# Layer norm with GELU: loads and stores on one DMA queue instead of two

## The chip, the cores and the metric

One NeuronCore of a Trainium2 chip; the other cores run nothing of this program. The metric is the device time in microseconds (us) of one execution. A kernel's time is the median over its timed runs. All runs compared here were in the fast state, at a granted clock of 1.0. Each of the last two experiments also had one run in the slow state, which is named there and left out. A *ring* is below what one queue has lined up on one of the 16 DMA engines; DMA engines are *in step* when they land a transfer at about the same time.

## The reference, cut to what matters

```python
# x: (8, 1024, 2048) float32; gamma, beta: (2048,)
mean = np.mean(x, axis=-1, keepdims=True)
var = np.var(x, axis=-1, keepdims=True)
out = gamma * (x - mean) / np.sqrt(var + eps) + beta
return 0.5 * out * (1 + np.tanh(np.sqrt(2 / np.pi) * (out + 0.044715 * out ** 3)))
```

67.1 MB are read and 67.1 MB are written.

## The kernel before

The 8192 rows are cut into 16 blocks of 4 MB (128 partitions, 4 rows of 2048 each). Five SBUF buffers hold blocks; a block is loaded, worked on in place and stored from the same buffer. SyncE issues the loads on its hardware DMA queue, ScalarE issues the stores on its own:

```python
def slot(b): return (b + SLOTS - 1) % SLOTS          # SLOTS = 5

# SyncE
for b in range(B):                                    # B = 16
    if stored(b):
        sy.wait_ge(s_store[s], stored(b))             # the buffer's last store has landed
    # b == 0 and b == SPLIT (3): four DMAs of one row per partition, else one of 4 MB
    sy.dma_start(out=xts[s], in_=xg[b]).then_inc(s_load[s], 16 * R)
...
# ScalarE, after the last GELU of block b
ins.then_inc(s_r, 1)
ac.dma_start(out=og[b], in_=xt)._wait_ge(s_r, b + 1).then_inc(s_store[slot(b)], 16)
ac.sem_inc(s_g, 1)
```

VectorE takes the statistics, GpSimd the reciprocal root, ScalarE normalises, VectorE multiplies by gamma, TensorE adds beta into PSUM, ScalarE applies GELU. The four rows of the last block are stored one by one.

## Time and profile before

| | before |
|---|---|
| median of 4 runs | 320.19 us (320.01 to 320.34) |
| span of the profiled run | 318.5 us |
| DMA queues, share of 16 engines | q1 (loads) 49.4%, q10 (stores) 49.0% |
| busiest compute engine | ScalarE 79% |

The prediction below quotes the page and the stretches. This is the DMA view of the kernel before from 304 us to the end of the span, in 40 slices of 0.36 us; the figures are GB/s.

```profile
GB/s 181 317 316 362 542 452 429 362 362 362 520 475 429 384 362 384 520 407 452 407 362 407 452 429 475 407 362 407 362 45 23 23 45 23 0 0 0 0 0 0
```

All 16 DMA engines work until about 314.5 us (29 slices). Then the rate is 23 to 45 GB/s. One engine alone moves an 8 KB packet in about 309 ns, 26.5 GB/s: what is left is one engine that is late. Its last packet ends at 316.57 us.

### The profile page before, as it was taken

To read this page: it belongs to the slowest core of one execution; us is meant where nothing else is said; L and a number is where in the kernel's file an instruction comes from. 1 tells how busy PE (TensorE), PEld (TensorE's weight loads), DVE (VectorE), ACT (ScalarE), POOL (GpSimd) and SP (SyncE) were. 2 spreads that over 40 slices of the span, in tenths; PEclk is the share of its full clock that TensorE was granted. 3 is DMA by queue.
4 is the path that set the end of the run, shared out by engine and by line. 5 is a ranking of instruction groups with operands and counts; after the bars stand their busy time and mean duration, and the time that the engine had idled before them with its cause. 6 is when DMAs were issued, how large, how long until landed. Compare 5 with 4: busy or idle time off the path is not lost.

```text
span 318.5 us, 2090 instructions
## 1 busy us (share of the span) xinstructions
PE 244.3 (77%) x520; PEld 57.2 (18%) x520; DVE 247.5 (78%) x386; ACT 251.7 (79%) x132; POOL 110.6 (35%) x201
## 2 busy tenths in 40 slices
PE   2769999999999989687795868958589595886860
PEld 1212222222212112111121112212112121111110
DVE  3499999999999897786968968599686986869810
ACT  2769999999999989698696967969589695995970
POOL 1144444444444444232443333333332433324300
DMA  7999999999999999999999999999999999999995
GB/s 289 438 457 401 394 434 430 444 424 436 432 424 444 417 453 416 440 440 416 457 403 457 420 436 444 411 461 403 453 432 424 449 407 457 424 432 403 453 396 209
DMA packets 6002, 134.26 MB, mean 421 GB/s; under 512 B 704, under 2 KB 752, under 8 KB 752
## 3 DMA queue, kind: packets, MB, share of 16 engines
q1 hardware_dynamic: 3168, 67.11, 49.4%
q10 hardware_dynamic: 2832, 67.13, 49.0%
q14 instruction: 2, 0.02, 0.0%
HBM read 67.13 MB, written 67.11 MB: 421 GB/s over the span
## 4 chain that ended last, share of the span: by engine, by line
DMA 64%; ACT 14%; DVE 10%; POOL 5%; PE 3%; issue 1%; ACTq 0%; DVEq 0%; POOLq 0%; SPq 0%
DMA xt<-in_x_dram 32%; DMA out_dram<-xt 30%; ACT yk L195 9%; DVE sts L149 7%; ACT xt L202 4%; POOL ves L135 3%; DVE zg L158 2%; PE ps L220 2%; DMA rows<-in_gamma_dram 2%; POOL rss L137 2%; POOL nms L139 1%; DVE mvs L155 1%; PE ps L237 1%; ACT g_t L191 1%; ACTq L205 0%
## 5 line engine op out<-in xcount | busy, mean ns | idle before, releaser
L149 DVE BATCH_NORM_STATS2 sts<-xt 128x6 f32<-128x512 f32 x256 | 157.7, 679 | 33.5 <-DMA xt<-in_x_dram 31.9
L195 ACT ACTIVATE yk<-xt,nms,rss 128x2048 bf16<-128x2048 f32 x64 | 133.7, 2090 | 48.9 <-POOL nms L139 42.9
L237 PE MATMUL ps<-zg,ident 128*128 128x512 bf16 x256 | 120.8, 627 | 55.8 <-DVE zg L158 54.7
L233 PE MATMUL ps<-b_hl,ones_b 33*128 33x512 bf16 x256 | 120.6, 624 | 2.2 <-PEq L228 2.2
L202 ACT ACTIVATE xt<-ps 128x2048 f32<-128x2048 f32 x64 | 118.9, 1858 | 1.5 <-PE ps L237 1.5
L135 POOL TENSOR_SCALAR ves<-mvs 128x1 f32<-128x1 f32 x64 | 38.5, 602 | 179.2 <-DVE mvs L155 179.2
L158 DVE TENSOR_TENSOR zg<-yk,g_t 128x2048 bf16<-128x2048 bf16 x64 | 76.5, 1195 | 19.2 <-ACT yk L195 19.2
L237 PEld LDWEIGHTS ps<-zg,ident 128*128 128x128 bf16 x256 | 27.6, 130 | 149.0 <-DVE zg L158 113.7
L233 PEld LDWEIGHTS ps<-b_hl,ones_b 33*128 33x128 bf16 x256 | 27.0, 127 | 92.1 <-issue 88.4
L139 POOL TENSOR_SCALAR nms<-mvs,rss 128x1 f32<-128x1 f32 x64 | 35.7, 558 | 6.3
L137 POOL TENSOR_TENSOR rss<-ves,mhalf 128x1 f32<-128x1 f32 x64 | 35.3, 552 | 5.3
L155 DVE BATCH_NORM_AGGREGATE mvs<-sts 128x2 f32<-128x24 f32 x64 | 16.9, 264 | 2.2
L220 PE MATMUL ps<-rows,ones 1*128 1x512 f32 x8 | 7.2, 1076 | 6.1 <-DMA rows<-in_gamma_dram 6.1
L188 ACT ACTIVATE b_hl<-rows 1x2048 bf16<-1x2048 f32 x1 | 1.9, 1909 | 5.3 <-DMA rows<-in_beta_dram 5.3
L166 DVE TENSOR_TENSOR b_hl<-rows,b_hl 1x2048 bf16<-1x2048 f32 x1 | 2.3, 2280 | 2.8 <-ACT b_hl L189 2.8
L220 PEld LDWEIGHTS ps<-rows,ones 1*128 1x128 f32 x8 | 2.5, 327 | 9.2 <-DMA rows<-in_gamma_dram 6.1
L191 ACT ACTIVATE g_t<-ps 128x2048 bf16<-128x2048 f32 x1 | 1.9, 1877 | 1.9 <-PE ps L220 1.9
L184 ACT ACT_TABLE_LOAD x1 | 1.3, 1283 | 0.9 <-SPq L107 0.9
L189 ACT ACTIVATE b_hl<-rows 1x2048 bf16<-1x2048 f32 x1 | 1.9, 1908 | 0.0
L161 DVE MEMSET b_hl<- 33x1024 uint32 x1 | 0.9, 912 | 1.2 <-SPq L107 1.2
L126 POOL MEMSET ones<- 65x128 f32 x1 | 0.2, 202 | 0.5 <-SPq L107 0.5
L130 POOL TENSOR_SCALAR_AFFINE_SELECT ident<-ident 128x128 bf16<-128x128 bf16 x1 | 0.3, 295 | 0.1
(7 smaller groups left out, 0.9 us busy)
## 6 DMA issues: line engine op xcount, KB each, us to landing
out_dram<-xt ACTq DMA_DIRECT2D x15, 4096.0 KB, 32.6
xt<-in_x_dram SPq DMA_DIRECT2D x14, 4096.0 KB
xt<-in_x_dram SPq DMA_DIRECT2D x8, 1024.0 KB, 8.4
out_dram<-xt ACTq DMA_DIRECT2D x4, 1024.0 KB, 8.6
rows<-in_beta_dram ACTq DMA_DIRECT2D x2, 8.0 KB, 5.9
rows<-in_gamma_dram ACTq DMA_DIRECT2D x1, 8.0 KB, 5.1
```

Of the source, the lines that this page charges most:

```text
L135: po.tensor_scalar(out=ves[:, c], in0=mvs[:, k, 1:2], scalar1=float(eps), scalar2=1.0, op0=ALU.add, op1=ALU.mult)._wait_ge(s_a, k + 1).the ...
L137: po.tensor_tensor(out=rss[:, c], in0=ves[:, c], in1=mhalf, op=ALU.pow)._wait_ge(s_q, 2 * k + 1).then_inc(s_q, 1)
L139: po.tensor_scalar(out=nms[:, c], in0=mvs[:, k, 0:1], scalar1=rss[:, c], scalar2=-1.0, op0=ALU.mult, op1=ALU.mult)._wait_ge(s_q, 2 * k + 2 ...
L149: ins = ve.bn_stats(out=sts[:, q, j, :], in_=xr[:, j, :])
L155: ve.bn_aggr(out=mvs[:, q], in_=sts[:, q])._wait_ge(s_o, count).then_inc(s_a, 1)
L158: ve.tensor_tensor(out=zgs[q % 2], in0=yks[q % 2], in1=g_t, op=ALU.mult)._wait_ge(s_n, count).then_inc(s_z, 1)
L191: ac.activation(out=g_t, in_=pss[0], func=ACT.Identity)._wait_ge(s_tg, 1).then_inc(s_c, 1)
L195: ac.activation(out=yks[t % 2], in_=xts[slot(b)][:, q], func=ACT.Identity, scale=rss[:, q:q + 1], bias=nms[:, q:q + 1])._wait_ge(s_p, t + ...
L202: ins = ac.activation(out=xt[:, q], in_=pss[i % 2], func=ACT.Gelu_apprx_tanh)._wait_ge(s_t, i + 1)
L220: ins = pe.matmul(pss[0][:, cols(j)], lhsT=ones[64:65], rhs=rows[64:65, j * K // nsub:(j + 1) * K // nsub, :d // K], start=True, stop=True)
L233: ins = pe.matmul(ps[:, cols(j)], lhsT=ones_b, rhs=b_hl[:, cols(j)], start=True, stop=False)
L237: ins = pe.matmul(ps[:, cols(j)], lhsT=ident, rhs=zgs[k % 2][:, cols(j)], start=False, stop=True)
```

## The change

All loads and all stores go to SyncE's queue, load b+4 behind store b; ScalarE issues no stores. Block 3's load becomes one DMA of 4 MB. The hardware loops of the other engines stay.

```diff
@@ SyncE
-                for b in range(B):
+                def load(b):
                     s = slot(b)
                     if stored(b):
                         sy.wait_ge(s_store[s], stored(b))
...
+                        sy.dma_start(out=xts[s], in_=xg[b]).then_inc(s_load[s], 16)
+                for b in range(SLOTS):
+                    load(b)
+                for b in range(B):
+                    s = slot(b)
+                    for q in range(R) if by_row(b) else (slice(None),):
+                        stores += 1
+                        c = slice(q, q + 1) if by_row(b) else q
+                        sy.dma_start(out=og[b, :, c], in_=xts[s][:, c])._wait_ge(s_r, stores).then_inc(s_store[s], 16)
+                    if SLOTS <= b + AHEAD < B:        # AHEAD = 4
+                        load(b + AHEAD)
@@ ScalarE
-                        ac.dma_start(out=og[b], in_=xt)._wait_ge(s_r, b + 1).then_inc(s_store[slot(b)], 16)
-                        ac.sem_inc(s_g, 1)
+                        ac.sem_inc(s_g, 1)._wait_ge(s_r, stores)
```

The intent: whole transfers in a row instead of loads and stores mixed by packets, and a ScalarE free of DMA issues.

More of the change, by code (lines that the diff above doesn't have):

```diff
@@ L12 @@
 SLOTS = 5
-SPLIT = 3
+AHEAD = 4
 K = 16
@@ L111, in _ @@
             def _(sy):
-                for b in range(B):
+                stores = 0
+                def load(b):
                     s = slot(b)
@@ L115, in _ @@
                         sy.wait_ge(s_store[s], stored(b))
-                    for q in range(R):
-                        if b == 0:
+                    if b == 0:
+                        for q in range(R):
                             sy.dma_start(out=xts[s][:, q:q + 1], in_=xg[0, :, q:q + 1]).then_inc(s_first[q], 16)
-                        elif b == SPLIT:
-                            sy.dma_start(out=xts[s][:, q:q + 1], in_=xg[b, :, q:q + 1]).then_inc(s_load[s], 16)
-                    if b not in (0, SPLIT):
-                        sy.dma_start(out=xts[s], in_=xg[b]).then_inc(s_load[s], 16 * R)
+                    else:
+                        sy.dma_start(out=xts[s], in_=xg[b]).then_inc(s_load[s], 16)
[9 more added lines that the diff above has]
+                        load(b + AHEAD)
             @block.gpsimd
@@ L152, in stats @@
                             if wait[0] is s_load[s]:
-                                ins.then_inc(s_load[s], -16 * R)
+                                ins.then_inc(s_load[s], -16)
                     ins.then_inc(s_o, 1)
@@ L175, in _ @@
                         s, q = divmod(k, R)
-                        stats(s, q, (s_load[s], 16 * R) if q == 0 else None, k + 1)
+                        stats(s, q, (s_load[s], 16) if q == 0 else None, k + 1)
                         scale((q - 1) % R, k + 1)
@@ L191, in _ @@
                 ac.activation(out=g_t, in_=pss[0], func=ACT.Identity)._wait_ge(s_tg, 1).then_inc(s_c, 1)
+                stores = 0
                 for t in range(T + 1):
@@ L202, in _ @@
                     ins = ac.activation(out=xt[:, q], in_=pss[i % 2], func=ACT.Gelu_apprx_tanh)._wait_ge(s_t, i + 1)
-                    if by_row(b):
+                    if by_row(b) or q == R - 1:
+                        stores += 1
                         ins.then_inc(s_r, 1)
-                        ac.dma_start(out=og[b, :, q:q + 1], in_=xt[:, q:q + 1])._wait_ge(
-                            s_r, b + q + 1).then_inc(s_store[slot(b)], 16)
-                        ac.sem_inc(s_g, 1)
-                    elif q == R - 1:
-                        ins.then_inc(s_r, 1)
-                        ac.dma_start(out=og[b], in_=xt)._wait_ge(s_r, b + 1).then_inc(s_store[slot(b)], 16)
-                        ac.sem_inc(s_g, 1)
+                        ac.sem_inc(s_g, 1)._wait_ge(s_r, stores)
                     else:
```

## The prediction

> **What bounds the kernel now.** I read the page first, busy shares, then the DMA queues, and after that the DMA traffic by stretch, the waits and the chain. No engine is the bound: the busiest three stand at 77 to 79%.
>
> ```profile
> PE 244.3 (77%) x520; PEld 57.2 (18%) x520; DVE 247.5 (78%) x386; ACT 251.7 (79%) x132; POOL 110.6 (35%) x201
> ...
> q1 hardware_dynamic: 3168, 67.11, 49.4%
> q10 hardware_dynamic: 2832, 67.13, 49.0%
> ...
> DMA 64%; ACT 14%; DVE 10%; POOL 5%; PE 3%; issue 1%; ACTq 0%; DVEq 0%; POOLq 0%; SPq 0%
> ```
>
> The two hardware queues (q1 holds SyncE's loads, q10 ScalarE's stores) together fill the 16 DMA engines for 98.4% of the span, half each, and the chain that ended last is 64% DMA. The question is thus only how fast the 16 engines drain 134 MB, and whether they are ever without work. The windows view, by stretch, tells both; its last two columns are the DMA share (over 1.00 by rounding of packets into stretches) and GB/s.
>
> ```profile
> 10.00:32.00 22.00, 16.43 (x33) 3.78 (x32) 17.81 (x26) 16.54 (x9) 6.95 (x12) 1.00 1.01 432
> 32.00:52.00 20.00, 18.38 (x41) 4.20 (x40) 18.76 (x31) 18.83 (x11) 7.98 (x13) 1.00 1.02 416
> 56.00:280.00 224.00, 179.55 (x388) 41.43 (x388) 185.28 (x293) 185.59 (x98) 83.22 (x145) 1.00 1.00 433
> 284.00:304.00 20.00, 14.69 (x33) 3.34 (x32) 15.43 (x24) 15.37 (x9) 6.54 (x12) 1.00 0.98 419
> 304.00:314.00 10.00, 3.73 (x9) 0.81 (x8) 1.22 (x1) 4.81 (x3) 0.00 (x0) 1.00 0.98 407
> 314.00:318.50 4.50, 0.00 (x0) 0.00 (x0) 0.00 (x0) 0.00 (x0) 0.00 (x0) 1.00 0.12 49
> ```
>
> From 10 to 32 us there are loads alone, on one queue: 432 GB/s. From 56 to 280 loads and stores alternate from two queues: 433 GB/s. So **one queue already runs as fast as two**. The slower stretches have causes of their own, treated below. The waits say how the queues are fed:
>
> ```profile
> SPq L122 <- DMA out_dram<-xt: 240.3, 11, 47.2
> ...
> DVE sts L149 <- DMA xt<-in_x_dram: 31.9, 11, 3.7
> ```
>
> SyncE spends 240 us waiting for a buffer's store to land before it reloads the buffer (11 times, blocks 5 to 15), and VectorE waits for 11 loads, 31.9 us in all. These waits look like an expensive loop: in the chain a store of 35 us, a load of 34 us, and 8.9 us of compute make 78 us for four blocks, 19.5 us a block. But the 35 and 34 us are queueing: about 3.5 transfers of 4 MB share engines that are busy all the time. The waits are the bound's shadow, not the bound.
>
> **The service time of one block.** The trace's packets of 32 KB take 1213 ns in mean as loads and 1215 ns as stores. A 4 MB transfer is 128 such packets, 8 on each DMA engine, so 8 x 1.213 = 9.70 us; block 1's load landed at 22.6 us on most engines and block 2's at 32.4, which agrees. A block in and out is 19.4 us; the landings into one buffer, five blocks apart, are 96.8 to 97.0 us apart, 19.4 per block. Compute needs less: ScalarE issued its first three stores at 36.02, 52.40 and 68.79 us, 16.4 us a block, while nothing held it up.
>
> **What the Trainium skill says.** "DMA: Bandwidth & Descriptors", section "Issuing engines are not separate DMA queues", says that DMAs of all issuing engines run on the same 16 DMA engines and interleave, and that several issuers save only sequencer time. The 432 against 433 GB/s agree. The same page, section "Queues, rings and completion order", says that each DMA engine alternates between the queues that have work by packets, and consumes one queue's descriptors in ring order. Both agree: a lone load takes 9.7 us here, and one among stores 30 us and more. That section also says that a completion's semaphore write lands only after that engine's earlier writes; the trace shows no stop for it between two loads (9.7 us apart) or between the stores of blocks 12 and 13 (285.1 to 294.8, 9.7 us). The page's table "Specifications" gives 435 GB/s as the fabric's ceiling: the trace's 432 to 433 is nearly that, so I leave no room for a faster transfer.
>
> **The change, part by part.**
> (1) *Stores move to SyncE's queue.* The same 19 store issues leave ScalarE, 339 ns each by the tile view, 6.4 us in all. ScalarE isn't the bound and waits for GpSimd 42.9 us in the kernel before; worth 0 on the path. SyncE has the time.
> (2) *Order.* Transfers are now strictly in a row: store b, load b+4, store b+1, load b+5. Bytes are the same, and so is packet time. Worth 0 if the queue never runs dry.
> (3) *Does it run dry?* I lay out the queue with 9.70 us per transfer. Loads 1 to 4 end at 22.7, 32.4, 42.1, 51.8; store 0 is issued at 36 and runs 51.8 to 61.5; store 1, issued at 52.4, runs to 71.2. Load 5 needs store 0 landed, with about 1 us for the slowest engine (the late landings of the trace): issued near 62.5, it has 8.7 us to spare, where an issue needs about 1 us to its first packet (first issue 0.93 us, first packet 1.92). Store 2 is computed at 68.8, needed at 80.9; store 3 at 85.2, needed at 100.3. Later a load is issued when the store of the block before lands, always with a load and a store (19.4 us) still ahead of it. A block's last row passes VectorE only after the next block's load has landed: store b can be issued 8.9 us after load b+1 (128.89 to 137.79 in the chain). In the new order four transfers, 38.8 us, lie between load b+1's end and store b's start. So the smallest slack is 8.7 us and the queue doesn't run dry.
> (4) *Block 3's load as one DMA in place of four.* Its 8 KB packets, 512 of them, took 10.76 us of each engine (mean 336 ns, beside the first store); as 32 KB packets it takes 9.70. This is the 416 GB/s of the stretch 32 to 52. Gain 1.06 us, on the bound.
> (5) *The tail.* Block 14's store was issued at 293.91, when block 13's was about to land (294.8 on most engines), and landed at 304.9: 10.1 us in place of 9.7, the DMA share of 0.98 in that stretch. In the new order load 15 ends at 275, so store 14 can be issued near 284 and is needed at 294: gain 0.4 us. The last block's rows are ready by 300 and needed from 304; four rows of 8 x 312 ns each are 10.0 us as before.
> (6) *The end.* One DMA engine is late: fifteen end by 314.7, the last at 316.57, and the span closes at 318.5. The same engine serves the same share: unchanged, 0.
>
> Sum: 320.14 - 1.06 - 0.4 = **318.7 us**.
>
> **The rivals.**
> *A. A bubble at every change of direction.* The kernel before has no ring on which a load follows a store: only load after load, store after store, or the two from different rings, where one ring's latency can hide behind the other's packet. With 13 or so loads among stores there are about 24 such changes. If each cost 0.3 us, it would be +7.2 us: 326 us, just slower than 2%; at 0.05 us, 1.2 us, 320. Against it: same-direction neighbours show no bubble though they too carry a semaphore write, and the alternating stretch runs full while changing direction at each packet. The trace can't exclude it, so it gets the tail of the range.
> *B. Head-of-line blocking.* SyncE stands at a store's wait while a load behind it could go. In the layout of (3) the slack is 8.7 us at the worst place. If compute were slower by more than that, the DMA would idle. Compute keeps 16.4 us against 19.4, so the lead grows until loads hold it. It would give 0 to +2 us if the start were tighter than laid out.
> *C. The stores and loads no longer fight, so the chain's 35 us becomes 10 and the kernel gets 20 us faster.* Transfers will land faster one by one, and waits on them will shrink, but the 98% share says that the engines have nothing to give. 134.2 MB at 433 GB/s are 310 us, plus 1.9 before the first packet, 1.9 for the late engine and 2.0 to the end: about 316, which is the floor of this program. A gain of 2% (313.7 us) is below it.
>
> **Range and chances.** The gains (4) and (5) sum to 1.5 us with little doubt about their size; the late engine may move by a microsecond either way; A at a few hundredths to 0.1 us adds up to 2.4. I put 8 times in 10 between 317.5 and 321.0. Faster by 2% would need what C lacks: 0.01. Slower by 2% (over 326.5) needs A at 0.3 us or more each, or B in every block: 0.04. Within 2%: 0.95.
>
> **What would show each step right or wrong.** In the DMA queues of the changed kernel one hardware queue should hold all 134 MB at 98 to 99%, and the other only gamma and beta. Issue to landing of a store should fall from a median of 32.6 us to 10 to 20. The stretch 32 to 52 should show about 432 GB/s, and 56 to 280 again 430 or more: a lower figure there is rival A if spread evenly over all blocks, rival B if idle stretches stand before late store issues on SyncE. VectorE's wait for loads should nearly vanish in the middle or just shift; it doesn't matter for the time. The prediction is wrong if a pair of store and load takes other than 19.4 us in the middle.

## The result, and the profile after

The changed kernel takes **322.01 us** (median of 4 runs, 321.26 to 322.72) against 320.19. The ratio is 1.0057, with a 95% interval of 1.0037 to 1.0077. Ratios here are the mean time of one kernel's fast runs over that of the other's of the same rounds, so not quite the ratio of the quoted medians. It is "the same" at the 2% level, but clearly slower, and outside the predicted range of 317.5 to 321.0.

The page of the changed kernel, for the lines that the prediction showed of the kernel before:

```profile
PE 244.3 (76%) x520; PEld 57.2 (18%) x520; DVE 248.2 (77%) x386; ACT 251.5 (78%) x132; POOL 113.4 (35%) x201
...
q1 hardware_dynamic: 5472, 134.22, 97.8%
q10 hardware_dynamic: 96, 0.02, 0.0%
...
DMA 47%; DVE 19%; ACT 15%; POOL 9%; PE 3%; issue 2%; SPq 0%; POOLq 0%; ACTq 0%; DVEq 0%
```

One queue carries everything and keeps the engines at 97.8%. The windows view, same stretches and columns as in the prediction (DMA share and GB/s last):

```profile
10.00:32.00 22.00, 16.42 (x33) 3.77 (x32) 17.86 (x26) 16.22 (x9) 6.95 (x12) 1.00 1.02 438
32.00:52.00 20.00, 18.38 (x41) 4.26 (x40) 18.76 (x31) 18.82 (x11) 8.03 (x14) 1.00 1.01 415
56.00:280.00 224.00, 184.01 (x398) 42.62 (x399) 187.85 (x295) 189.92 (x101) 87.19 (x148) 1.00 1.00 432
```

The middle runs at 432 GB/s, against 433. The stretch 32 to 52 is at 415 against 416: the slow spot that the prediction put down to the split load is still there **without the split load**. The waits of SyncE and VectorE:

```profile
SPq L122 <- DMA out_dram<-xt: 162.8, 11, 19.0
SPq L131 <- ACT xt L214: 126.0, 13, 30.8
...
DVE sts L160 <- DMA xt<-in_x_dram: 25.2, 9, 3.6
```

SyncE's waits for stores fell from 240 to 163 us, and its new waits for results are 126 us. Neither matters, since the queue had work all that time. The loss is at the end. The DMA view of the changed kernel from 304 us to the end, slices of 0.415 us:

```profile
GB/s 434 336 493 454 355 454 494 336 434 454 395 415 415 415 454 395 415 454 415 395 494 434 296 198 79 59 99 79 79 79 79 99 39 39 59 0 0 0 0 0
```

The common rate ends at about 313.7 us, *earlier* than before. But then some 79 GB/s go on for 3 us, and some 40 after that: 79 is three engines at 26.5 GB/s. Their last packets end at 317.37, 318.50 and 318.78 us. So the common end moved from about 314.6 to 313.7 us (-0.9), the distance from there to the last engine from 1.9 to 5.1 us (+3.2), and the span by +2.1 (318.5 to 320.6).

**When the lateness arises** can be read from the trace's landing records. Each large DMA here has 16 landing records, one per DMA engine; they don't say which engine. I call the last of the 16 minus their median the *lateness* of that DMA (L is a load, S a store, the number is the block), in us:

| | L2 | L4 | L8 | L12 | L15 | S14 |
|---|---|---|---|---|---|---|
| before | 0.63 | 1.03 | 1.03 | 1.71 | 2.24 | 2.22 |
| after | 0.83 | 2.05 | 3.03 | 4.11 | 4.90 | 4.95 |

In the changed kernel it grows throughout, and by steps. After 60 us, 44 of its packets took over 1253 ns (the usual 1213 and 40 more), 9.05 us too long in sum, which is about the drift of three engines. Of the 44, 24 end within 0.45 us before a load's landing: they are an engine's *last* packet of a load that stands before a store. Most of the others are one or two packets before that. Laid end to end, the packets form 16 chains, one per engine: some 35 of the 44, 7.0 us, lie on three of them. In the kernel before there are 17 such packets, 1.6 us in sum, and 1 of them ends a load.

The kernel before has another way to a late engine. Between 140 and 290 us it has no packet over 1253 ns, yet its lateness grows from 1.03 us at L8 to 2.24 at L15. The packets of 1216 to 1253 ns in that time make up for it: 106 packets, 62 of them of stores, 1.3 us too long in sum, most of them on one engine. What makes that engine a little slow is not known.

### The profile page after: what moved, and what is told of

It is laid out like the page before. It is cut to its first block, busy times and chain, and to the rows that moved or that the text cites. A ratio compares the mean times of both kernels' runs of the same rounds, so it can differ in the third digit from the quotient of the medians.

```text
span 320.6 us, 2087 instructions
## 1 busy us (share of the span) xinstructions
PE 244.3 (76%) x520; PEld 57.2 (18%) x520; DVE 248.2 (77%) x386; ACT 251.5 (78%) x132; POOL 113.4 (35%) x201
## 3 DMA queue, kind: packets, MB, share of 16 engines
q1 hardware_dynamic: 5472, 134.22, 97.8%
## 4 chain that ended last, share of the span: by engine, by line
DMA 47%; DVE 19%; ACT 15%; POOL 9%; PE 3%; issue 2%; SPq 0%; POOLq 0%; ACTq 0%; DVEq 0%
DMA out_dram<-xt 36%; DVE sts L160 12%; ACT yk L207 12%; DMA xt<-in_x_dram 9%; DVE zg L169 6%; POOL ves L146 5%; POOL rss L148 3%; PE ps L227 2%; ACT xt L214 2%; DMA rows<-in_gamma_dram 2%; POOL nms L150 1%; DVE mvs L166 1%; PE ps L244 1%; ACT g_t L202 1%; SPq L122 0%
## 5 line engine op out<-in xcount | busy, mean ns | idle before, releaser
L146 POOL TENSOR_SCALAR ves<-mvs 128x1 f32<-128x1 f32 x64 | 41.0, 641 | 171.4 <-DVE mvs L166 171.4
## 6 DMA issues: line engine op xcount, KB each, us to landing
out_dram<-xt SPq DMA_DIRECT2D x15, 4096.0 KB, 34.6
```

What stands on the lines that cost most here:

```text
L146: po.tensor_scalar(out=ves[:, c], in0=mvs[:, k, 1:2], scalar1=float(eps), scalar2=1.0, op0=ALU.add, op1=ALU.mult)._wait_ge(s_a, k + 1).the ...
```

## The experiments

The theories. **D**: on one ring, DMA engines that are a little behind the others lose time when they pass from a load to a store, so their lateness grows, and the last of them sets the end. **Step 4 of the prediction**: the split of block 3's load costs 1 us. **F**: one queue makes some engines late whatever the order. **I**: the lateness comes from loads issued on the landing of the slowest engine, with stores waiting behind them on SyncE. More came up on the way. Twelve kernels ran, all with correct results.

### Two queues, without the split

```diff
-                        elif b == SPLIT:
-                            sy.dma_start(out=xts[s][:, q:q + 1], in_=xg[b, :, q:q + 1]).then_inc(s_load[s], 16)
-                    if b not in (0, SPLIT):
+                    if b != 0:
```

> The kernel before with one part of the change alone: block 3's load as one DMA. Step 4 of the prediction: 1.06 us faster, 319.1 us. New theory: the slow 8 KB packets of block 3's load around 38 to 41 us are slow because the first store starts then, and the changed kernel shows the same one-off loss of about 0.8 us at its own first store near 50 us on 32 KB packets; then the loss is paid here too, by 32 KB packets, and only the 0.2 us of smaller packets is gained: 319.9 to 320.1 us.

Measured: 319.91 us (319.76 to 319.98), ratio 0.9989, interval 0.9976 to 1.0003. This is what the new reading said, and not step 4, which said 319.1. The windows view of this kernel:

```profile
32.00:52.00 20.00, 18.40 (x41) 4.28 (x40) 18.77 (x31) 18.84 (x11) 8.03 (x14) 1.00 1.00 417
56.00:280.00 224.00, 184.88 (x400) 42.75 (x400) 187.04 (x296) 190.01 (x101) 84.72 (x148) 1.00 1.00 433
```

417 GB/s again in the slow stretch. With the split, 8 KB packets of block 3's load between 33 and 51 us took 0.82 us per engine too long; without it, 22 large packets at 37 to 49 us do, 0.66 us per engine; in the changed kernel it is 0.84 us per engine near 50 us. In each kernel this is the time at which the first store starts. The lateness of this kernel is 1.86 us at L12 and 2.65 at S14. It has the one-DMA load of the changed kernel and two queues: so it is **the queue, not the split, that the changed kernel pays for**.

### One queue, with the split

```diff
+                    elif b == SPLIT:
+                        for q in range(R):
+                            sy.dma_start(out=xts[s][:, q:q + 1], in_=xg[b, :, q:q + 1]).then_inc(s_load[s], 16)
```

> The changed kernel with block 3's load by rows again, so the move to one queue alone. Theory D (drift): three DMA engines fall behind by 4 to 5 us through slow packets at the changes from a load to a store on one ring, and the split has little to do with it: 322.2 us, with fifteen to thirteen engines done near 313.9 and the last near 318.8. If step 4 was right as it stood, the split costs 1 us: 323.1 us.

Measured: 322.43 us (322.28 to 323.09), ratio 1.0076. The move to one queue alone gives the loss. It also shows what the split itself costs while no store runs: block 3's load landed 9.95 us behind block 2's by rows (medians 32.45 and 42.40), and 9.72 us behind it as one DMA in the changed kernel (32.50 and 42.22). That is 0.2 us, where step 4 said 1.06. The DMA view from 304 us to the end shows late engines again, here two and then one:

```profile
GB/s 434 375 454 474 355 434 474 375 474 415 415 395 415 434 434 395 454 434 415 415 474 395 395 138 39 59 59 39 59 59 39 59 20 20 39 0 0 0 0 0
```

Its lateness goes 0.60 (L2), 1.08 (L4), 2.67 (L8), 4.16 (L12), 4.98 (L15), nearly the series of the changed kernel.

### Stores and loads in pairs

```diff
-                    if SLOTS <= b + AHEAD < B:
-                        load(b + AHEAD)
+                    if b % 2 == 1:
+                        for n in (b + AHEAD - 1, b + AHEAD):
+                            if SLOTS <= n < B:
+                                load(n)
```

> One queue, but stores and loads in pairs: two stores, then two loads, so that a load stands before a store 7 times instead of 12. Theory D: the lateness of the last engine against the first (now 5 us, of which 1.8 us in the kernel before too) shrinks by some 5/12 of its 3.2 us growth, 1.3 us: 320.7 us. Rival F (one queue for all traffic makes some engines late whatever the order, per packet): no change, 322.0 us.

Measured: 321.34 us (321.12 to 321.90), ratio 1.0036: better than the changed kernel, less than D said. The time is not clean: store 14 was issued at 294.8 us, just as the queue ran empty, and landed at 305.9 instead of 304.4. But the landing series is the best evidence, because here some loads stand before a load and others before a store:

```
load before a load :  L6 2.53   L8 2.53   L10 2.97   L12 3.25   L14 3.56
load before a store:  L7 2.54   L9 2.91   L11 3.20   L13 3.55   L15 4.00
```

From the load to its partner (L6 to L7, L8 to L9, ...) the lateness grows by 0.01, 0.38, 0.23, 0.30 and 0.44 us, 1.36 in sum. From the load before a store to the next pair's first load (L5, at 2.57, to L6, L7 to L8, ...), across two stores, it changes by -0.04, -0.01, 0.06, 0.05 and 0.01. So **in this kernel lateness grows in the load that precedes a store on the ring, and hardly anywhere else**. F falls as the explanation of this growth; a run below shows one engine that loses time in stores.

### Load b+3 instead of b+4

```diff
-AHEAD = 4
+AHEAD = 3
```

> One queue, load b+3 behind store b in place of load b+4: SyncE then waits for a store that landed some 19 us earlier and no load is issued at the moment when the latest engine lands. The number of changes from load to store stays 12. Theory D: 322 us, last engine 4 to 5 us late as before. Rival I (the late engines come from loads issued late, on the landing of the slowest engine, and stores behind them on SyncE): lateness back to 1.8 us, 319 to 320 us.

Measured: 323.15 us (322.90 to 323.40), ratio 1.0094, which neither theory said. The order itself costs time at the end: the last load now lands one transfer later (284.9 us), so store 14 was issued only at 298.5 us, while store 13 had landed at 294.6 on most engines, which then stood idle for some 5 us. The DMA view of this kernel from 304 us, slices of 0.43 us:

```profile
GB/s 1226 0 0 1226 0 0 1226 0 0 1226 0 134 479 307 537 383 364 537 326 422 498 307 517 403 307 575 345 383 517 326 498 422 307 537 383 0 0 0 0 0
```

The pattern 1226, 0, 0 is 16 packets that start together, every 1.2 us: the engines are in step here, and end together. By the time at which store 14 came, the last of them had about run dry too, and that wipes the lateness out. But until then it grows as in the changed kernel: 0.37 (L2), 1.36 (L4), 2.58 (L8), 3.95 (L12), 4.66 (L15), though no load waited for a landing that had just come. So I falls by the series, not by the time.

### Halves in turn, and halves together

Each 4 MB transfer is cut in two of 2 MB. In the first kernel the order is half store, half load, half store, half load; in the second store, store, load, load.

```diff
+                    for h in range(H):                # H = 2
+                        store(b, half(h), b + 1)
+                        if more:
+                            if h == 0:
+                                ready(n)              # wait for the buffer's last store
+                            load(n, h)
```

> One queue; each 4 MB transfer cut in two of 2 MB (16 KB packets), in the order half store, half load, half store, half load: 23 changes from load to store in place of 12. Theory D (late engines lose a little at each such change, in the last runs 0.26 to 0.35 us per change for the latest): 11 changes more, 3 us more lateness, 325 us. Rival S (the loss depends on time or bytes, not on changes): 322 us as in the changed kernel, beside a few tenths for smaller packets.

> Control of the run before: the same halves in the order store, store, load, load, so 12 changes from load to store with the same packets and the same number of transfers. Both theories: 322 to 322.5 us; the difference between the two runs is what 11 changes cost.

Measured: in turn 322.51 us (322.14 to 322.75, ratio 1.007); together 324.44 us (324.31 to 324.64, ratio 1.0132). **The sign is opposite to D as it stood**: nearly twice as many changes, and 1.9 us faster. Rival S (322 us for both) fits the first kernel and misses the control by 2 us, as did D. About 1 us in both is the smaller packets: store 14's landing has its median at 305.44 us in both, and at 304.41 in the changed kernel. The DMA views from 304 us, first in turn (slices of 0.42 us), then together (0.465 us):

```profile
GB/s 392 314 432 471 334 491 432 373 432 432 412 432 412 451 432 392 451 432 392 432 451 392 451 432 451 275 137 157 137 98 137 78 59 59 0 0 0 0 20 0
```

```profile
GB/s 458 317 423 423 440 388 493 370 458 405 423 405 458 388 440 405 458 405 440 423 423 458 335 141 70 88 88 70 88 70 70 35 18 35 18 0 0 0 0 18
```

The common rate ends near 314.5 us in both; the difference is the tail. The landings say why. From here on I measure how far the last engine is behind the *first* of the 16. In turn, it was 0.95 us behind at the start, 3.68 us at 114 us, and 3.76 at 304 us: **it stopped falling behind**, through some 16 further changes. Together, it went on to 5.66 us. So the loss is not a fee for each change: with the shorter turns there was a distance behind the others at which the engine lost no more.

### Half of the engines shifted on purpose

An extra load of 8 partitions runs on 8 DMA engines alone: after four of them, 8 of the 16 landings of load 2 came 4.85 us or more behind the first. Put behind load 1, they make these 8 engines late from the start. The data are overwritten by block 4's load, which waits for them.

```diff
                 for b in range(SLOTS):
+                    if b == 2:
+                        for k in range(4):
+                            sy.dma_start(out=xts[slot(4)][8 * k:8 * k + 8], in_=xg[4, 8 * k:8 * k + 8]).then_inc(s_x, 16)
+                    if b == 4:
+                        sy.wait_ge(s_x, 64)
                     load(b)
```

> The changed kernel with four extra loads[...] (8 partitions each, one packet of 32 KB per engine), so that half of the engines run 4.85 us behind the other half from the start; slower by design. Theory D as I now read it (an engine loses time when it passes from load to store while the others are already storing): the whole late half goes on falling behind, from 4.85 us to some 7 or 8 us at the end: 326 us or more. Rival P (some particular engines are slow at the change, in step or not): the late half as a whole stays 4.85 us behind, and only two or three engines fall further: 322 to 327 us by whether those lie in the late half; told apart by the landings, where the middle of the late half moves or doesn't.

Measured: 336.12 us (two runs), ratio 1.0496. Much of it is an accident of my extra loads. The windows view of this kernel:

```profile
10.00:20.00 10.00, 5.94 (x11) 1.38 (x10) 6.98 (x9) 5.15 (x3) 1.69 (x3) 1.00 1.07 456
22.00:38.00 16.00, 14.45 (x33) 3.26 (x31) 15.02 (x24) 14.84 (x9) 6.80 (x12) 1.00 1.06 145
40.00:52.00 12.00, 7.38 (x16) 1.68 (x16) 5.62 (x10) 8.02 (x5) 1.89 (x4) 1.00 1.00 431
```

While the extra loads ran, most packets took some 3.9 us in place of 1.21, and on *all* engines: load 2's first landing came at 44.0 us, against 32.2 in the changed kernel. What followed is still of use: the late half landed 4.85 to 5.88 us behind at L2 and, but for one engine at 7.69, 4.92 to 5.83 behind at S14. The middle of the late half rose from 5.05 us to 5.7 by L8 and then stayed: far less was lost than the 2 to 3 us that D said, and the run taken alone speaks for rival P. The engines did not stall together at the first store either (one packet over 1.26 us between 42 and 113 us, against 18 long ones near 50 us in the changed kernel). The one engine that went on falling behind did so **in stores**: from 5.87 us at L7 to 7.69 at S14, about 0.15 us in each store and almost nothing in the loads. So not all lateness comes before a store; this is like the late engine of the kernel before.

The next two took the 8 partitions four apart, with two extra loads and with four:

```diff
+                            sy.dma_start(out=xts[slot(4)][k:32:4], in_=xg[4, k:32:4]).then_inc(s_x, 16)
```

> The changed kernel with two extra loads (8 partitions each, four apart, so that the 8 DMA engines do not crowd on the same few partitions as in the run with four): 8 engines carry 2 packets more and start 2.43 us behind. Theory D2 (after the runs with halves and with the shift: an engine that passes from load to store a little after the others loses time there, until it is some 4 to 5 us behind, and then no more): the whole late half drifts from 2.4 to 4 to 5 us, and the kernel takes 321.5 to 323 us. Rival P (two or three particular engines lose, whatever the others do): the late half stays at 2.4 us in its middle and only single engines drift; time 322 to 325 us. The middle of the late half in the landings tells them apart.

> The same with four extra loads, 4.85 us: 8 engines carry 4 packets, 4.85 us, more work than in the changed kernel. Theory D2: at this distance nothing is lost at the changes, and no burst of 16 first stores either, so the late half stays 4.85 us behind, the latest engine at 5.5 to 6.5: main engines end at 313.2, the last at 319, kernel 321 to 322.5 us, no slower than the changed kernel in spite of the extra packets. If losses go on at any distance: 324 us and more.

Measured with two: 323.99 us (323.51 to 324.94, ratio 1.011). The late half was 2.39 to 3.16 us behind at L2 and 4.71 to 5.91 at S14, but for one engine at 7.25. **A whole half of the engines drifted, only because it was put a little behind**: this loss isn't a trait of two or three particular engines, and rival P falls here. The time is 1 us over what D2 said.

Measured with four: 327.43 us (326.56 to 328.01, ratio 1.0213), well over D2's 321 to 322.5. The late half stood still from L6 (5.37 to 6.92 us behind) to L9 (5.31 to 6.94), but lost before and after, to 6.65 to 9.11 at S14. So the distance at which nothing is lost is **not** simply 5 us; D2's second half falls, and the time fits "if losses go on at any distance". The crowding was gone, as the windows view of this kernel shows for the same stretch:

```profile
22.00:38.00 16.00, 14.45 (x33) 3.33 (x32) 14.89 (x23) 14.83 (x9) 6.92 (x12) 1.00 1.00 430
```

### An early small store

Two queues without the split, and one store of 64 KB in the first microseconds, to see whether the 0.8 us at the first store can be paid early.

```diff
+                ac.dma_start(out=og[B - 1, :, 0, :128], in_=warm)._wait_ge(s_w, 1).then_inc(s_wd, 16)
+                ac.wait_ge(s_wd, 16)
```

> Two queues, block 3's load as one DMA, and one store of 64 KB to the output in the first microseconds. If the 0.8 us that every engine loses at the first store belongs to the first store of the program as such, it is taken then, beside the start, and packets near 38 us stay at 1213 ns: 319.1 to 319.6 us against 319.9 without the early store. If it belongs to a burst of stores beginning, or to the addresses, it stays: 319.9 us.

Measured: 320.16 us (320.01 to 320.28, ratio 0.9997). It doesn't help: slow packets stand at 39 to 41 us as without it (0.95 us per engine with one at 50 us). It is not the program's first store as such; a beginning burst or the addresses are not told apart.

### Half of the stores moved

Stores of even blocks on SyncE's queue, those of odd blocks on ScalarE's.

```diff
+                    if b % 2 == 0:
+                        sy.dma_start(out=og[b], in_=xts[s])._wait_ge(s_r, b + 1).then_inc(s_store[s], 16)
```

> Half of the move: stores of even blocks on SyncE's queue behind their loads, those of odd blocks on ScalarE's queue as in the kernel before. If a change from load to store on one ring is what makes engines late, and a second ring's packets hide it, the lateness of the last engine comes back to 2 to 2.7 us and the time to 320.0; if such changes cost by their number alone, half of the loss stays: 321 us.

Measured: 323.74 us in the middle of three fast runs, scattered from 322.26 to 324.14, ratio 1.009 (1.0052 to 1.0128); a fourth run, 328.42, counts as slow. The run tells nothing of the question. Stores 0 and 1 shared the engines, so store 0 landed late, and loads 5 and 6 were issued only then, as the DMA issues of SyncE show (start, length):

```profile
72.19 0.33 SPq L122 DMA_DIRECT2D xt<-in_x_dram  x1
72.57 0.62 SPq L129 DMA_DIRECT2D out_dram<-xt  x1
73.40 29.36 SPq L122 DMA_DIRECT2D xt<-in_x_dram  x2
```

In the changed kernel load 5 went out at 64.30 us. Here the queues ran nearly dry around 72 us, and that was my ordering. One thing can be read from it: after that, packets were long again, 16 that start at 73 us (0.74 us per engine) and 22 that start at 81 to 83 us (1.03 us per engine). So the stall seen at the first store is not confined to it.

### Quarters in turn

`H = 4` in the first of the two kernels with halves.

> One queue, transfers of 1 MB (8 KB packets) in strict turns of store and load: 45 changes from load to store, each engine changing direction every 2.5 us, nearer to what two queues do by packets. Packets of 8 KB cost every engine more: 309 ns each against 1213 / 4, for 232 - 32 large packets' worth some 5 us, so the engines in step should end near 319 instead of 313.7. Theory D3 (an engine out of step is held back at changes only until it is most of one turn behind; the run with halves stopped at 3.75 us for turns of 4.85 us): the latest engine stays within about 2.5 us, and the kernel takes 323 to 324 us. If every change costs the late engines anew, lateness passes 5 us and the kernel takes 326 us or more.

Measured, on another chip than the other experiments (the kernel before took 320.33 us there): 329.79 us in the middle of three fast runs, scattered from 327.03 to 330.36, ratio 1.0261; a fourth run, 333.04, counts as slow. Again spoiled by supply, so the time decides nothing between the two theories. Load b+4 is issued when store b-1 has landed, and with quarters only two transfers of 2.5 us are in the queue behind that store, so the engines catch up with SyncE, whose issues then take up to twice as long (DMA issues of SyncE in this kernel, at 124 and at 245 us):

```profile
124.19 0.49 SPq L124 DMA_DIRECT2D xt<-in_x_dram  x1
...
245.52 0.92 SPq L124 DMA_DIRECT2D xt<-in_x_dram  x1
```

The slow packets stand in these bursts, at 64 to 69, 223 to 230, 243 to 247 and 264 to 270 us. Between 80 and 200 us they are all but absent, at a mean of 309 to 310 ns. Until 184 us the last engine stays 1.7 to 1.9 us behind the first, through some 20 changes from load to store; then it loses another 0.5 us. So a change from load to store does not by itself cost an engine time.

## Why the prediction was wrong, point by point

- **What bounds it: right.** The DMA engines do, in both kernels.
- **Steps 1 to 3 (issues, order, whether the queue runs dry): right.** Load 5's landing has its median at 81.7 us and load 15's at 275.4: 19.37 us per block, where 19.4 were laid out. For the engines in step there is no bubble.
- **Step 4 (1.06 us for block 3's load): wrong.** The load was slow by that much, but the split is only 0.2 us of it (the run with one queue and the split). The rest belongs to the start of the first store and is there without the split: 0.82, 0.66 and 0.84 us per engine in three kernels. Dropping the split on two queues gave 0.3 us (319.91 against 320.23 us, not clear of noise), with step 5 in it. I had seen the slow packets in the one load that was special and not asked what else was special at that time.
- **Step 5 (0.4 us in the tail): right.** Store 14 landed 9.7 us behind store 13 (medians 294.7 and 304.4), not 10.1. It was issued at 289.2 us, not 284, since load 15 lands late on the late engines, but still in time. The new order is not needed for it: two queues without the split have the 9.7 us too (294.4 and 304.1).
- **Step 6 ("One DMA engine is late ... unchanged, 0"): this is the step that failed.** The distance from the common end to the last engine went from 1.9 to 5.1 us. The reasoning "the same engine serves the same share" took lateness for a matter of work. Here it was a matter of order: with loads and stores on one ring, three engines fell behind, mostly in loads that stand before a store. The range allowed the late engine one microsecond either way; it took 3.2.
- **Rival A (a bubble at each change of direction)** named the right place and the wrong payer. The engines in step, 13 of 16, pay nothing after the first change; the late ones pay up to some 0.7 us at a change (the longest packet took 1.92 us), by uneven steps, and the kernel waits for the latest. Its 326 us for 0.3 us a change are 1.8%, not over 2%.
- **Rivals B and C: rightly put aside.** No idle of the queue and no gain of 20 us.
- **What would show it:** that a store's time from issue to landing would fall to 10 to 20 us was wrong, without effect; it is 34.6, since stores wait in the queue behind the transfers issued before them. The stretch 32 to 52 stayed at 415 GB/s, where 432 was to show step 4 right. The last sign, a pair other than 19.4 us, stayed quiet at 19.37: it looks at the engines in step, and the loss was with the others. Its 1213 ns as a mean of the packets is the median; the mean is 1214 to 1215, with no effect.

Sum by the common engines and the late ones: predicted -1.5 and 0, measured -0.9 and +3.2.

**What stays open.** Shown: one queue makes engines late, with the split or without; lateness grows at changes from load to store on one ring (pairs); being behind is enough to be hit (shift by two); it can stop growing at some distance (halves in turn, most engines in the shift with four crowded loads). Several forecasts of times missed all the same, so this is where the loss arises and not yet a law for its size. Not shown: what in the hardware holds back an engine that ends its load while others already store; why the late half drifted with four loads in one kernel and not in the other; and why a second ring hides it. That packets of the other ring fill in is a guess: the run meant for it was spoiled.

Of all kernels run, two queues without the split is the fastest, 319.91 us, and its interval still touches 1.

## What to carry to other kernels

Where a kernel is bound by DMA, look at the last microseconds of the DMA view: here the latest of the 16 DMA engines set the end, and a rate of a small multiple of 26.5 GB/s was that many engines still at work. Mean rate and share hardly show it (421 and 419 GB/s over the span). Keep loads and stores on two queues where nothing else speaks against it: one queue was as fast for most engines here, and made some late. When a stretch is slow, ask for all that happens at that time before blaming the one odd instruction in it.

## What the Trainium skill lacked or had wrong

- "DMA: Bandwidth & Descriptors", section "Issuing engines are not separate DMA queues": it says that issuing from several engines saves only sequencer time. Here the queue itself mattered a little: one against two, both without the split, gives ratios of 1.0057 and 0.9989 to the same kernel, and 4.95 against 2.65 us of lateness.
- The same page, section "Queues, rings and completion order", tells how the engines take packets from rings; nothing there says that an engine behind the others loses time between a load and a store on one ring. Here up to some 0.7 us at one change, 9.05 us in sum over all engines, most of it on three.
- The same page, section "The descriptor swizzle", tells which partitions an engine writes in a transfer of 128 partitions. It lacks what loads of 8 adjacent partitions do to all other traffic beside them: 145 GB/s for 16 us, against 430 with the 8 partitions four apart.
- No page that I read has the stall when large stores first begin: 0.66 to 0.84 us per engine in three kernels, not removed by an early store of 64 KB, and a like one stands later in the run with half of the stores moved.
